# Start of a hybrid decoder block: x fetched first, weights scaled instead of x, half of the scale sums on TensorE

## The chip, the cores and the metric

The kernel runs on one core of a Trainium2 chip. The metric is device time in microseconds (us) for one execution of the whole kernel. Engines: TensorE (PE in the profile: matmuls and transposes; its weight loads are PEld), VectorE (DVE), ScalarE (ACT), GpSimd (POOL) and SyncE (SP). SP does no arithmetic; its queue issues most of the transfers (DMAs) from memory. Every engine runs its own list of instructions in order and waits on semaphores for the others.

## The reference, cut to what matters

One decoder layer on x of 512 tokens by 2048, all fp32. A conditioning vector c makes six rows of 2048 numbers; two of them act on the first normalisation:

```python
mod = (silu(c) @ w_ada + b_ada)                  # w_ada: 2048 x 12288
shift1, scale1, gate1, shift2, scale2, gate2 = split(mod, 6)
h = rms_norm(x, norm1_w) * (1.0 + scale1) + shift1
proj = h @ w_in                                  # w_in: 2048 x 7168
# aq, ak, av (attention), gq, gf, gi, gg (gated recurrence) are columns of proj;
# attention and recurrence, output projection, residual, and an MLP of width 8192 follow
```

So the first large product needs the row scale1 (a product of a vector with a 2048 x 2048 matrix), the norm of every token of x, and x with its features on the partitions.

## The kernel before, in words

The 2048 features are 16 tiles of 128, counted by k; two neighbouring k are a pair, named by its first, k0. Every fp32 operand of a large matmul is split into a rounded high part (fp32r) and the remainder, and a product is made of three matmuls: high by high, high by low, low by high. `_split` does it for weights (L39 on ACT the high part whi, L40 on DVE the low part wlo); the parts of x are hhi and hlo.

The columns of `w_in` are taken in groups. The first group is 512 columns from 4096 (the forget gate) and 256 from 3072 (gq), six 128-column tiles, accumulated over the 16 k in six PSUM banks: 18 matmuls of 128x512 for each k. The second group (`first_groups(4096 + 512, 3072 + 256, ...)`) is the same shape. In both, x carries only the scale; the shift is added later through its own product with `w_in` (`shift_through`). From the third group on, x carries scale and shift, and TensorE's order is written out by hand; that part is outside the change.

What has to be there before the first group:

- g1c, the column form of norm1_w * (1 + scale1). It is made in eight blocks of 256 columns (two k each) by `mod_cols`: `gemv` fetches the block's 2048x256 piece of `w_ada` in eight DMAs on SP (L125) and DVE multiplies the sixteen k pieces by sc = silu(c) and adds them up in two accumulators (L130 for the first two, L132 for fourteen). `to_cols` transposes them (L152, tile pc) and ACT sums over the former partitions (L155); L170 and L172 on DVE add the bias and form the product. Block b serves k = 2b and 2b + 1.
- x: sixteen 128x512 tiles xs (L262 on SP), squares (L271 on ACT, L268 on DVE), the root (L218 on DVE, L219 on POOL), the scaling by rx (L284 ACT, L286 DVE), transposes on TensorE (L290) and ACT's copy out of PSUM (L292), which gives the tiles xnT.
- `scaled(k)`: ACT multiplies xnT[k] by g1c (L342) and rounds it to hhi (L343), DVE makes hlo (L344).

`first_groups` goes over the pairs: `scale_block(k0)` (the weighted sums of the *next* block and `scaled` for both k), then `load_w` (L195, one DMA of 512 KB and one of 256 KB on SP), the splits and the matmuls (`ch_mm`, L213 to L215). At the last pair, `shift_start` begins the vector products of the shift in the background (`bg_step`). In this part the order of the instructions on each engine is made by a scheduler from dependences and priorities, not by the order of the text.

Of the kernel before, what the change touches and what calls it, by code (L numbers as in the profile page):

```python
# [8 lines left out]
F32 = mybir.dt.float32  # L9
# [3 lines left out]
ALU = mybir.AluOpType  # L13
# [21 lines left out]
def _split(nc, pool, src, n=512, eng=None):  # L35

    hi = pool.tile([P, 512], F32R, name="whi", tag="whi")[:, 0:n]
    lo = pool.tile([P, 512], F32R, name="wlo", tag="wlo")[:, 0:n]
    nc.scalar.copy(hi, src)  # L39
    _split.low = (eng or nc.vector).tensor_tensor(lo, src, hi.bitcast(F32), op=ALU.subtract)  # L40
    return hi, lo
# [3 lines left out]
def hybrid_block(ctx, tc, x, c, positions, norm1_w, w_ada, b_ada, w_in, q_norm_w, k_norm_w,  # L45
# [30 lines left out]

    crow = ca.tile([P, P], F32, name="crow", tag="rows")
    nc.sync.dma_start(crow[0:NK], c[0].rearrange("(r p) -> r p", p=P))
    nc.sync.dma_start(crow[NK:2 * NK], norm1_w[0].rearrange("(r p) -> r p", p=P))
    nc.sync.dma_start(crow[2 * NK:P], b_ada[0].rearrange("(r p) -> r p", p=P))  # L80
# [6 lines left out]
    sc = const.tile([P, NK], F32, name="sc")  # L87
# [30 lines left out]
    def gemv(view, vec, col0, n=512, early=False):  # L118
# [72 lines left out]
    def load_w(view, k0, c0, n=512, eng=None, ahead=True, raws=None, behind=False, cast_behind=False):  # L191
        with tc.high_priority() if ahead else ExitStack():
# [5 lines left out]
            with tc.issue_after(evacuated[0].ins) if cast_behind and evacuated else ExitStack():  # L198
                return [_split(nc, wr, raw[:, j], n, eng if j else None) for j in range(2)]
# [51 lines left out]
    hhi, hlo, spare = [], [], []  # L251


    first_scale = mod_cols(1, 0, g1c, n1c, 256, True)
    for _ in range(8):
        next(first_scale)
    xs = [[slot("xs") for _ in range(4)] for _ in range(NT)]
    ssx = sm.tile([P, NT, 4], F32, name="ssx", bufs=1)
    rx = sm.tile([P, NT], F32, name="rx", bufs=1)
    for q in range(4):  # L260
        for ti in range(NT):
            nc.sync.dma_start(xs[ti][q], x_t[:, ti, q * 512:(q + 1) * 512])  # L262
    for q in range(4):
        for ti in range(NT):
            jk = work("jk")
            with tc.issue_after(sc_ready.ins), tc.issue_after(sig_ready.ins):
                if q == 3 and ti % 2:
                    dve.tensor_tensor_reduce(jk, xs[ti][q], xs[ti][q], op0=ALU.mult, op1=ALU.add, scale=1.0, scalar=0.0,  # L268
                                             accum_out=ssx[:, ti, q:q + 1])
                else:  # L270
                    act.activation(jk, xs[ti][q], AF.Square, accum_out=ssx[:, ti, q:q + 1])  # L271
    dve.tensor_reduce(rx, ssx, axis=AX.X, op=ALU.add)
    rstd_of(rx, rx, NT, 1.0 / D)
    run_all(first_scale)
    second_scale = mod_cols(1, 1, g1c, n1c, 256, True)
    spare.extend((hp0, hp1)[k % 2].tile([P, 512], F32, name="araw", tag=f"{c}{k}")
                 for k in range(8, NK) for c in ("hi", "lo"))
    for _ in range(8):
        next(second_scale)
    xnT = []  # L280
    for q in range(4):
        for ti in range(NT):
            if q == 0 and ti % 2 == 0:
                act.activation(xs[ti][q], xs[ti][q], AF.Copy, scale=rx[:, ti:ti + 1])  # L284
            else:
                dve.tensor_scalar(xs[ti][q], xs[ti][q], rx[:, ti:ti + 1], None, op0=ALU.mult)  # L286
# [1174 lines left out]
```

## Time and profile before

| | us |
|---|---|
| median of three runs | 2255.97 (2255.27 to 2257.48) |
| the profiled execution | 2254.72 |
| its span, first to last instruction | 2252.8 |
| PE busy, of the span | 2205.3 (98%) |
| DVE busy | 1807.0 (80%) |
| ACT busy | 1096.5 (49%) |
| POOL busy | 440.5 (20%) |
| first matmul of the first group | 37.24 |
| first matmul of the second group | 121.82 |

The profile is of one execution; its own time is 1.25 us below the median. Busy shares over 2250 us say little about the first 122, so the stretches of that part are read for themselves. "Idle before, releaser" at a row's end names what the engine waited for. The last three numbers of a row of the windows table are the granted TensorE clock (1.00 is full speed, 2.4 GHz), the busy share of the DMA engines and the GB/s that they moved.

### The profile page before, as it was taken

Reading aid. Unit: us, or ns where it says so; the run is one execution under the profiler, and the core shown is the slowest. Engines: PE = TensorE matmul, PEld = TensorE weight load, DVE = VectorE, ACT = ScalarE, POOL = GpSimd, SP = SyncE. Lnnn points to the kernel's source line nnn. Section 1 sums busy time; section 2 is a strip of 40 time slices with the busy share of each in tenths; the row PEclk is TensorE's granted clock in tenths of the full one; section 3 lists DMA queues with packets and bytes.
Section 4 is the critical chain, followed back from the end, with each engine's and each line's share of the span. In section 5 each row is a group of like instructions: output and inputs, shape, how many; then the busy total and the mean of one; then the engine's idle time right before and its main releaser. Section 6 shows DMA issues by size and latency. Waiting matters only on the chain.

```text
span 2252.8 us, 33043 instructions
## 1 busy us (share of the span) xinstructions
PE 2205.3 (98%) x11769; PEld 1823.7 (81%) x11769; DVE 1807.0 (80%) x2765; ACT 1096.5 (49%) x1950; POOL 440.5 (20%) x664
## 2 busy tenths in 40 slices
PE   4999999999999999999999999999999999999999
PEld 3788888888888888888888888888888888888887
DVE  6998878677976566778658988998897779967878
ACT  5555345443453564457545565565654333443332
POOL 1000022000210000003232322232332222222221
PEclk9999999999999999999999999999999999999999
DMA  9797655556555248738879789889989987998884
GB/s 322 261 330 263 212 182 161 172 187 211 174 182 170 76 157 293 259 110 287 319 283 361 294 295 387 317 299 354 345 287 358 372 316 258 341 348 315 307 294 165
DMA packets 262581, 598.30 MB, mean 266 GB/s; under 512 B 23220, under 2 KB 43968, under 8 KB 262416
## 3 DMA queue, kind: packets, MB, share of 16 engines
q1 hardware_dynamic: 186800, 332.54, 43.4%
q0 software_dynamic: 70720, 254.21, 30.7%
q10 hardware_dynamic: 4896, 9.44, 1.3%
q8 instruction: 93, 1.52, 0.3%
q14 instruction: 72, 0.59, 0.1%
HBM read 518.49 MB, written 77.61 MB: 265 GB/s over the span
## 4 chain that ended last, share of the span: by engine, by line
PE 79%; DVE 7%; issue 6%; DMA 6%; POOL 1%; ACT 1%; SPq 0%; POOLq 0%; DVEq 0%; ACTq 0%
PE f L1219 12%; PE f L1217 12%; PE f L1218 12%; PE prj L205 8%; PE prj L207 8%; PE prj L206 8%; PE f L215 2%; PE f L214 2%; PE f L213 2%; PE prj L213 2%; PE prj L214 2%; PE prj L215 2%; DMA f_lod<-fs 1%; DMA Fl<-f_lod 1%; DVE acc L132 1%
## 5 line engine op out<-in xcount | busy, mean ns | idle before, releaser
L1201 ACT CAST vhi<-raw 128x1024 fp32r<-128x1024 f32 x392 | 413.3, 1055 | 519.2 <-PE f L1219 408.8
L1202 DVE TENSOR_TENSOR vlo<-raw,vhi 128x1024 fp32r<-128x1024 f32 x392 | 476.2, 1224 | 139.6 <-ACT vhi L1201 139.2
L1219 PE MATMUL f<-vhi,Fl 128*128 128x512 f32 x1376 | 536.0, 390 | 0.8 <-DMA Fl<-f_lod 0.8
L1218 PE MATMUL f<-vlo,Fh 128*128 128x512 f32 x1376 | 536.3, 390 | 0.5 <-DVE vlo L1202 0.4
L1217 PE MATMUL f<-vhi,Fh 128*128 128x512 f32 x1376 | 536.3, 390 | 0.0
L39 ACT CAST whi<-wraw 128x512 fp32r<-128x512 f32 (+1 forms) x368 | 219.5, 602 | 418.9 <-PE prj L207 273.7
L40 DVE TENSOR_TENSOR wlo<-wraw,whi 128x512 fp32r<-128x512 f32 (+1 forms) x368 | 245.5, 672 | 165.1 <-ACT whi L39 157.3
L205 PE MATMUL prj<-whi,hi 128*128 128x512 f32 x896 | 360.0, 402 | 0.6 <-ACT aq L414 0.5
L207 PE MATMUL prj<-whi,lo 128*128 128x512 f32 x896 | 350.3, 391 | 0.1
L206 PE MATMUL prj<-wlo,hi 128*128 128x512 f32 x896 | 349.4, 390 | 0.0
L1218 PEld LDWEIGHTS f<-vlo,Fh 128*128 128x128 f32 x1376 | 258.4, 188 | 55.1 <-DVE vlo L1202 2.1
L1219 PEld LDWEIGHTS f<-vhi,Fl 128*128 128x128 f32 x1376 | 258.4, 188 | 54.8 <-DMA Fl<-f_lod 1.2
L1217 PEld LDWEIGHTS f<-vhi,Fh 128*128 128x128 f32 x1376 | 258.4, 188 | 53.3
L1185 DVE TENSOR_TENSOR raw<-raw,raw 128x1024 f32<-128x1024 f32 x224 | 271.0, 1223 | 3.4 <-DMA raw<-in_w_ff_dram 3.0
L132 DVE SCALAR_TENSOR_TENSOR acc<-araw,sc,acc 128x512 f32<-128x512 f32 (+1 forms) x392 | 251.0, 677 | 24.3 <-DMA araw<-in_w_ada_dram 23.8
L207 PEld LDWEIGHTS prj<-whi,lo 128*128 128x128 f32 x896 | 168.2, 188 | 36.7 <-DVE lo L247 0.6
L205 PEld LDWEIGHTS prj<-whi,hi 128*128 128x128 f32 x896 | 168.4, 188 | 35.1 <-ACT ak L414 0.9
L206 PEld LDWEIGHTS prj<-wlo,hi 128*128 128x128 f32 x896 | 168.6, 188 | 32.6
L1163 POOL DMA_DIRECT2D Fh<-f_hid x112 | 79.0, 705 | 426.9 <-PE f L1219 409.3
L215 PE MATMUL f<-hi,wlo 128*128 128x512 f32 x256 | 100.0, 391 | 1.1 <-DVE wlo L40 1.1
L213 PE MATMUL f<-hi,whi 128*128 128x512 f32 x256 | 100.4, 392 | 0.0
L214 PE MATMUL f<-lo,whi 128*128 128x512 f32 x256 | 99.7, 390 | 0.0
(311 smaller groups left out, 2905.8 us busy)
## 6 DMA issues: line engine op xcount, KB each, us to landing
raw<-in_w_ff_dram SPq DMA_DIRECT2D x224, 512.0 KB, 10.5
araw<-in_w_ada_dram SPq DMA_DIRECT2D x384, 256.0 KB, 4.5
Fh<-f_hid POOLq DMA_DIRECT2D x112, 512.0 KB, 6.8
Fl<-f_lod POOLq DMA_DIRECT2D x112, 512.0 KB, 8.1
wraw<-in_w_in_dram SPq DMA_DIRECT2D x104, 512.0 KB, 4.9
Fh<-h_hid POOLq DMA_DIRECT2D x60, 512.0 KB, 6.4
Fl<-h_lod POOLq DMA_DIRECT2D x60, 512.0 KB, 7.7
f_hid<-part POOLq DMA_DIRECT2D x48, 512.0 KB, 7.2
```

What stands on the lines that cost most here:

```text
L39: nc.scalar.copy(hi, src)
L40: _split.low = (eng or nc.vector).tensor_tensor(lo, src, hi.bitcast(F32), op=ALU.subtract)
L132: dve.scalar_tensor_tensor(acc, raw[:, k - k0], vec[:, k:k + 1], acc, op0=ALU.mult, op1=ALU.add)
L205: pe.matmul(banks[ti], lhsT=hi[:, ts], rhs=whi, start=first, stop=False)
L206: pe.matmul(banks[ti], lhsT=hi[:, ts], rhs=wlo, start=False, stop=False)
L207: pe.matmul(banks[ti], lhsT=lo[:, ts], rhs=whi, start=False, stop=last)
L1185: dve.tensor_tensor(dst, a, b, op=ALU.subtract)
L1201: cast_done.append(act.copy(hi, src))
L1202: split_done.append(dve.tensor_tensor(lo, src, hi.bitcast(F32), op=ALU.subtract))
L1217: pe.matmul(banks[t], lhsT=fh[u][a][:, ts], rhs=whi[:, a], start=first, stop=False)
L1218: pe.matmul(banks[t], lhsT=fh[u][a][:, ts], rhs=wlo[:, a], start=False, stop=False)
L1219: pe.matmul(banks[t], lhsT=fl[u][a][:, ts], rhs=whi[:, a], start=False, stop=end)
```

## The change

- **x first.** The three small loads of c, norm1_w and the bias go to ACT's queue. SP's first sixteen issues are x, then block 0, pair 0, block 1, pair 2, blocks 2 to 7. The pairs from 4 on are issued on POOL's queue.
- **Weights scaled, x not.** `_split` takes a scale: ACT rounds weight times g1c[k] (L43 of the new kernel), DVE makes the low part with one scalar_tensor_tensor (L44). x goes into the matmuls of both first groups without g1c; `shifted` applies scale and shift to it later.
- **Sums on TensorE.** Blocks 0, 1, 3 and 5 are *summed*: sc stands in the first of 32 columns of a zeroed operand scz, and sixteen matmuls (128x32 by 128x256, fp32) accumulate the k pieces in four strips of 32 partitions of one bank; ACT copies it, two transposes follow (L819), and DVE reduces. Blocks 2, 4, 6 and 7 are *gathered*: sixteen passes on DVE as before (L834, L836), then the old `to_cols` (now L159, L162).
- **Written order.** In this stage PE, SP, ACT and DVE follow the order of the text. For each pair: the parts of x of the next pair, the DVE passes of a gathered next block, the 18 matmuls of the first k, for a summed next block its 16 matmuls, 12 matmuls of the second k, the transposes of the next block's sum (`next_scale`), the last six matmuls, the splits of the next pair's weights. Tiles 8 to 15 of x are transposed at k0 = 2 and 6.
- A Sigmoid on a zeroed tile is run first, and one background piece list is started with 16 steps at the end where there were 12.

The diff, without lines that only rename or carry over:

```diff
-def _split(nc, pool, src, n=512, eng=None):
+def _split(nc, pool, src, n=512, eng=None, scale=None):
 
     hi = pool.tile([P, 512], F32R, name="whi", tag="whi")[:, 0:n]
     lo = pool.tile([P, 512], F32R, name="wlo", tag="wlo")[:, 0:n]
-    nc.scalar.copy(hi, src)
-    _split.low = (eng or nc.vector).tensor_tensor(lo, src, hi.bitcast(F32), op=ALU.subtract)
+    if scale is None:
+        nc.scalar.copy(hi, src)
+        _split.low = (eng or nc.vector).tensor_tensor(lo, src, hi.bitcast(F32), op=ALU.subtract)
+    else:
+        nc.scalar.activation(hi, src, AF.Copy, scale=scale)
+        _split.low = nc.vector.scalar_tensor_tensor(lo, src, scale, hi.bitcast(F32), op0=ALU.mult, op1=ALU.subtract)
...
-    nc.sync.dma_start(crow[0:NK], c[0].rearrange("(r p) -> r p", p=P))
-    nc.sync.dma_start(crow[NK:2 * NK], norm1_w[0].rearrange("(r p) -> r p", p=P))
-    nc.sync.dma_start(crow[2 * NK:P], b_ada[0].rearrange("(r p) -> r p", p=P))
+    act.dma_start(crow[0:NK], c[0].rearrange("(r p) -> r p", p=P))
+    act.dma_start(crow[NK:2 * NK], norm1_w[0].rearrange("(r p) -> r p", p=P))
+    act.dma_start(crow[2 * NK:P], b_ada[0].rearrange("(r p) -> r p", p=P))
...
-                return [_split(nc, wr, raw[:, j], n, eng if j else None) for j in range(2)]
+                return [_split(nc, wr, raw[:, j], n, eng if j else None, None if gain is None else gain[:, k0 + j:k0 + j + 1])
+                        for j in range(2)]
...
-            wt = load_w(win_v, k0, c_f, ahead=False)
-            wc = load_w(win_v, k0, c_q, 256, None, ahead=False)
+            wt = load_w(win_v, k0, c_f, ahead=False, gain=g1c)
+            wc = load_w(win_v, k0, c_q, 256, None, ahead=False, gain=g1c)
...
-    def scale_block(k0):
-        if k0 == 0:
-            run_all(second_scale)
-        elif k0 < 14:
-            run_all(mod_cols(1, k0 // 2 + 1, g1c, n1c, 256, True))
-        for k in (k0, k0 + 1):
-            scaled(k)
...
-    def scaled(k):
-        for l, t in zip((hhi, hlo), pair(k)):
-            l.append(t)
-        act.activation(xnT[k], xnT[k], AF.Copy, scale=g1c[:, k:k + 1])
-        act.copy(hhi[k], xnT[k])
-        dve.tensor_tensor(hlo[k], xnT[k], hhi[k].bitcast(F32), op=ALU.subtract)
-
     def shifted(k):
-        act.activation(hhi[k], xnT[k], AF.Identity, bias=s1c[:, k:k + 1])
-        act.activation(xnT[k], xnT[k], AF.Identity, bias=s1c[:, k:k + 1])
+        for d in (hhi[k], xnT[k]):
+            act.activation(d, xnT[k], AF.Identity, scale=g1c[:, k:k + 1], bias=s1c[:, k:k + 1])
...
+    def first_stage(c_f, c_q):
+
+        order = mybir.EngineType
+        with tc.manual_schedule(engines={order.PE, order.SP, order.Activation, order.DVE}):
+            return first_steps(c_f, c_q)
...
+        scz = slot("scz").rearrange("p (k m) -> p k m", m=32)
+        pool.memset(scz, 0.0)
...
+        on_pe = (0, 1, 3, 5)
...
+        def fetch_pair(k0):
+            wraws[k0] = []
+            for c, n in ((c_f, 512), (c_q, 256)):
+                raw = wr.tile([P, 2, n], F32, name="wraw", tag="raw", bufs=4)
+                (pool if k0 > 2 else nc.sync).dma_start(raw, win_v[:, k0:k0 + 2, c:c + n])
+                wraws[k0].append(raw)
+
+        def split_w(k):
+            parts[k] = [_split(nc, wr, raw[:, k % 2], raw.shape[2], None, g1c[:, k:k + 1]) for raw in wraws[k - k % 2]]
+
+        def split_x(ks):
+            for k in ks:
+                hl = pair(k)
+                hhi.append(hl[0])
+                hlo.append(hl[1])
+                split_to(hl, xnT[k])
...
+        def turn_x(q, j, tag="bg"):
+            pt = bank("ptx", tag=tag)
+            for ti in range(NT):
+                pe.transpose(pt[:, ti * P:(ti + 1) * P], xs[ti][q][:, j * P:(j + 1) * P], ident)
+            t = slot("xnT")
+            (dve.tensor_copy if q == 1 else act.copy)(t, pt)
+            xnT.append(t)
+
+        def summed(b, rounds):
+            if b not in accs:
+                accs[b] = bank("gp")
+            for r in rounds:
+                for j in range(4):
+                    k = 4 * r + j
+                    pe.matmul(accs[b][32 * j:32 * j + 32, 0:256], lhsT=scz[:, k], rhs=raws[b][k // 2][:, k % 2],
+                              start=r == 0, stop=r == 3)
+
+        def summed_out(b):
+            t = work("acc")[:, 0:256]
+            act.copy(t, accs[b][:, 0:256])
+            pc = bank("pc")
+            for j in range(2):
+                pe.transpose(pc[:, j * P:(j + 1) * P], t[:, j * P:(j + 1) * P], ident)
+            dve.tensor_reduce(g1c[:, 2 * b:2 * b + 2], pc[:, 0:256].rearrange("p (j a m) -> p j a m", j=2, m=32)[:, :, :, 0],
+                              axis=AX.X, op=ALU.add)
+            finish_scale(b)
+
+        def finish_scale(b):
+            d = g1c[:, 2 * b:2 * b + 2]
+            dve.tensor_tensor(d, d, bcol[:, NK + 2 * b:NK + 2 * b + 2], op=ALU.add)
+            mod_cols.last = dve.scalar_tensor_tensor(d, d, 1.0, n1c[:, 2 * b:2 * b + 2], op0=ALU.add, op1=ALU.mult)
+
+        def gathered(b):
+            accs[b] = [work("acc")[:, 0:256] for _ in range(2)]
+            for k in range(NK):
+                raw, acc = raws[b][k // 2][:, k % 2], accs[b][k % 2]
+                if k < 2:
+                    dve.tensor_scalar(acc, raw, sc[:, k:k + 1], None, op0=ALU.mult)
+                else:
+                    dve.scalar_tensor_tensor(acc, raw, sc[:, k:k + 1], acc, op0=ALU.mult, op1=ALU.add)
+
+        def gathered_out(b):
+            for _ in to_cols(accs[b], g1c[:, 2 * b:2 * b + 2]):
+                pass
+            finish_scale(b)
...
+        fetch_block(0)
+        fetch_pair(0)
+        scale_x(0, (0, 1))
+        summed(0, (0, 1))
+        turn_x(0, 0, "mm")
+        turn_x(0, 1, "mm")
+        scale_x(1, ())
+        split_x((0,))
+        summed(0, (2, 3))
+        summed_out(0)
+        turn_x(0, 2, "mm")
+        turn_x(0, 3, "mm")
+        fetch_block(1)
+        fetch_pair(2)
+        for j in range(4):
+            turn_x(1, j, "mm")
+        split_w(0)
+        split_x((1,))
+        split_w(1)
+        fetch_block(2)
+        split_x((2, 3))
+
+        bt = [bank("prj", tag="mm") for _ in range(4)]
+        bc = [bank("prc") for _ in range(2)]
+
+        def dense(k, between=None):
+            fine, coarse = parts.pop(k)
+            first, last = k == 0, k == NK - 1
+            for n, (hs, w) in enumerate(((hhi, 0), (hlo, 0), (hhi, 1))):
+                for banks, ws in ((bt, fine), (bc, coarse)):
+                    for j in range(len(banks)):
+                        pe.matmul(banks[j], lhsT=ws[w][:, j * P:(j + 1) * P], rhs=hs[k], start=first and n == 0,
+                                  stop=last and n == 2)
+                if n == 1 and between:
+                    between()
+
+        def next_scale(b):
+            if b in on_pe:
+                summed_out(b)
+            elif b < 8:
+                gathered_out(b)
+
+        for k0 in range(0, NK, 2):
+            b = k0 // 2 + 1
+            if k0 + 4 < NK:
+                fetch_pair(k0 + 4)
+            if k0 in (0, 4):
+                scale_x(2 + k0 // 4, range(NT))
+            if 0 < k0 < NK - 2:
+                split_x((k0 + 2, k0 + 3))
+            if b < 8 and b not in on_pe:
+                gathered(b)
+            dense(k0)
+            if b in on_pe:
+                summed(b, range(4))
+            if k0 in (2, 6):
+                turn_x(2 + k0 // 6, 0)
+                turn_x(2 + k0 // 6, 1)
+            dense(k0 + 1, lambda: next_scale(b))
+            if k0 in (2, 6):
+                turn_x(2 + k0 // 6, 2)
+                turn_x(2 + k0 // 6, 3)
+            if b + 2 < 8:
+                fetch_block(b + 2)
+            for k in (k0 + 2, k0 + 3):
+                if k < NK:
+                    split_w(k)
+        for _ in range(16):
+            bg_step()
+        return bt, bc
...
-    bt, bc = first_groups(4096, 3072, scale_block, shift_start)
+    xnT = []
+    bt, bc = first_stage(4096, 3072)
```

The order of the instructions on three engines follows from it. First SP at the start of the program, before (araw is a piece of `w_ada`, wraw a pair of `w_in`, xs is x):

```order
L78 DMA crow<-in_c_dram 16x128
L79 DMA crow<-in_norm_w_dram 16x128
L80 DMA crow<-in_b_ada_dram 96x128
L125 DMA araw<-in_w_ada_dram 128x2x256 x8
L262 DMA xs<-in_x_dram 128x512 x16
L125 DMA araw<-in_w_ada_dram 128x2x256 x8
L195 DMA wraw<-in_w_in_dram 128x2x512
L195 DMA wraw<-in_w_in_dram 128x2x256
L125 DMA araw<-in_w_ada_dram 128x2x256 x8
```

and of the changed kernel:

```order
L845 DMA xs<-in_x_dram 128x512 x16
L760 DMA araw<-in_w_ada_dram 128x2x256 x8
L767 DMA wraw<-in_w_in_dram 128x2x512
L767 DMA wraw<-in_w_in_dram 128x2x256
L760 DMA araw<-in_w_ada_dram 128x2x256 x8
L767 DMA wraw<-in_w_in_dram 128x2x512
L767 DMA wraw<-in_w_in_dram 128x2x256
L760 DMA araw<-in_w_ada_dram 128x2x256 x48
```

x has moved from behind block 0 to the first place; of the pairs only 0 and 2 are left on this queue.

Second DVE, where one block's sum ends and another begins, before (L170 and L172 finish g1c; lo is a low part of x):

```order
L344 TENSOR_TENSOR lo_578<-xnT,hi_577 128x512
L132 SCALAR_TENSOR_TENSOR acc<-araw,sc,acc 128x256
L344 TENSOR_TENSOR lo_583<-xnT,hi_582 128x512
L170 TENSOR_TENSOR g1c<-g1c,bcol 128x2
L132 SCALAR_TENSOR_TENSOR acc<-araw,sc,acc 128x256
L130 TENSOR_SCALAR acc<-araw,sc 128x256 x2
L132 SCALAR_TENSOR_TENSOR acc<-araw,sc,acc 128x256
L172 SCALAR_TENSOR_TENSOR g1c<-g1c,n1c 128x2
L132 SCALAR_TENSOR_TENSOR acc<-araw,sc,acc 128x256 x8
L344 TENSOR_TENSOR lo_687<-xnT,hi_686 128x512
```

and of the changed kernel from the last splits of pair 2 (k0 = 2) to the first of pair 4:

```order
L44 SCALAR_TENSOR_TENSOR wlo<-wraw,g1c,whi 128x512
L44 SCALAR_TENSOR_TENSOR wlo<-wraw,g1c,whi 128x256
L255 TENSOR_TENSOR lo_544<-xnT,hi_543 128x512
L255 TENSOR_TENSOR lo_548<-xnT,hi_547 128x512
L834 TENSOR_SCALAR acc<-araw,sc 128x256 x2
L836 SCALAR_TENSOR_TENSOR acc<-araw,sc,acc 128x256 x14
L826 TENSOR_TENSOR g1c<-g1c,bcol 128x2
L827 SCALAR_TENSOR_TENSOR g1c<-g1c,n1c 128x2
L44 SCALAR_TENSOR_TENSOR wlo<-wraw,g1c,whi 128x512
L44 SCALAR_TENSOR_TENSOR wlo<-wraw,g1c,whi 128x256
```

Before, the passes of a block are mixed with low parts and the finishing steps; now all low parts of the step stand ahead, the sixteen passes in one piece, and the finishing steps after them.

Third TensorE around the transposes of a gathered block (L152 before, L159 now), before, in the step of k0 = 4:

```order
L213 MATMUL prj<-hi_686,whi 128x512 x4
L152 MATMUL pc<-ident,acc 128x128
L214 MATMUL prj<-lo_687,whi 128x512 x4
L152 MATMUL pc<-ident,acc 128x128 x3
L215 MATMUL prj<-hi_686,wlo 128x512 x4
L213 MATMUL prc<-hi_686,whi 128x512
L214 MATMUL prc<-lo_687,whi 128x512
```

and of the changed kernel, in the second k of k0 = 2:

```order
L883 MATMUL prj<-hi_428,whi 128x512 x4
L883 MATMUL prc<-hi_428,whi 128x512 x2
L883 MATMUL prj<-lo_429,whi 128x512 x4
L883 MATMUL prc<-lo_429,whi 128x512 x2
L159 MATMUL pc<-ident,acc 128x128 x4
L883 MATMUL prj<-hi_428,wlo 128x512 x4
L883 MATMUL prc<-hi_428,wlo 128x512 x2
L800 MATMUL ptx<-ident,xs 128x128 x8
L883 MATMUL prj<-hi_543,whi 128x512 x4
```

Before, the four transposes are spread among the matmuls of the step's first k; now they stand as one behind the twelve matmuls with hi and lo of the second k, with six matmuls and eight transposes of x behind them.

## Rows read from the trace of the kernel before

**Rows 1.** Windows table of core 0: stretch, length, busy us (instructions), clock, DMA:

```profile
0.00:37.24 37.24, 7.33 (x37) 5.74 (x37) 19.21 (x54) 17.51 (x46) 9.63 (x24) 1.00 0.93 303
...
52.94:62.84 9.90, 9.90 (x37) 8.00 (x37) 9.90 (x26) 4.71 (x11) 0.00 (x0) 0.83 1.10 354
94.66:121.82 27.16, 27.16 (x115) 21.77 (x115) 21.38 (x67) 15.85 (x31) 0.00 (x0) 0.94 0.29 85
121.82:187.00 65.18, 65.18 (x296) 53.87 (x295) 60.47 (x109) 37.38 (x86) 5.29 (x9) 1.00 0.95 339
187.00:2252.80 2065.80, 2055.27 (x11090) 1701.69 (x11088) 1648.81 (x2392) 992.32 (x1712) 425.55 (x631) 1.00 0.75 263
```

**Rows 2.** Waits of PE in 0 to 190 us: total, times, longest:

```profile
PE ptx L290 <- ACT xs L284: 12.8, 1, 12.8
...
PE prj L213 <- ACT hi L343: 7.1, 4, 4.1
```

**Rows 3.** Timeline of SP's DMA issues, 0 to 35 us:

```profile
2.11 5.63 SPq L125 DMA_DIRECT2D araw<-in_w_ada_dram  x8
7.78 13.11 SPq L262 DMA_DIRECT2D xs<-in_x_dram  x16
```

**Rows 4.** Timeline of the x-norm chain on ACT:

```profile
25.57 0.63 ACT L271 ACTIVATE jk<-xs 128x512 f32<-128x512 f32 x1 [0.42 <-DMA xs<-in_x_dram]
...
29.16 1.33 ACT L284 ACTIVATE xs<-xs,rx 128x512 f32<-128x512 f32 x2 [2.87 <-POOL rx L219]
```

**Rows 5.** Timeline of DVE: weighted sums of block 0:

```profile
13.75 2.46 DVE L132 SCALAR_TENSOR_TENSOR acc<-araw,sc,acc 128x256 f32<-128x256 f32 x6 [1.40 <-DMA araw<-in_w_ada_dram]
```

**Rows 6.** Groups by line and shape, 0 to 122 us: busy, mean ns:

```profile
L40 DVE TENSOR_TENSOR wlo<-wraw,whi 128x512 fp32r<-128x512 f32 x18 | 12.6, 699 | 2.4 <-ACT whi L39 2.1 <-PE pc L152 0.3
...
L342 ACT ACTIVATE xnT<-xnT,g1c 128x512 f32<-128x512 f32 x16 | 10.8, 718 | 5.2 <-DVE g1c L172 5.2
...
L292 ACT COPY xnT<-ptx 128x512 f32<-128x512 f32 x16 | 8.4, 615 | 2.8 <-PE ptx L290 2.8
L132 DVE SCALAR_TENSOR_TENSOR acc<-araw,sc,acc 128x512 f32<-128x512 f32 x10 | 7.7, 774 | 0.0
...
L40 DVE TENSOR_TENSOR wlo<-wraw,whi 128x256 fp32r<-128x256 f32 x17 | 7.2, 434 | 1.2 <-ACT whi L39 1.2
...
L155 ACT ACTIVATE pc<-pc 128x256 f32<-128x256 f32 x16 | 5.9, 367 | 2.5 <-PE pc L152 2.2
...
L155 ACT ACTIVATION_READ_ACCUMULATOR pc<-pc 128x1 f32 x16 | 3.0, 190 | 0.0
```

**Rows 7.** Timeline of PE: steady matmuls, then sixteen transposes:

```profile
117.74 0.39 PE L213 MATMUL prj<-hi,whi 128*128 128x512 f32 x1
117.96 0.39 PE L214 MATMUL prj<-lo,whi 128*128 128x512 f32 x1
...
43.57 1.91 PE L290 MATMUL ptx<-ident,xs 128*128 128x128 f32 x16
```

**Rows 8.** Timeline of PE: 128x32 strips, 128x256 fp32 matmuls and neighbours:

```profile
252.37 0.39 PE L207 MATMUL prj<-whi,lo 128*128 128x512 f32 x1
252.69 0.46 PE L585 MATMUL pA<-gq,kk 128*32 128x32 f32 x32
252.96 1.02 PE L585 MATMUL pA<-z 128*32 128x32 f32 x96
253.91 0.51 PE L205 MATMUL prj<-whi,hi 128*128 128x512 f32 x1
...
277.10 1.02 PE L685 MATMUL pE<-z 128*128 128x256 f32 x4
```

**Rows 9.** Timeline of PE after two waits; windows row of a slow stretch:

```profile
52.94 1.70 PE L213 MATMUL prj<-hi,whi 128*128 128x512 f32 x4 [1.97 <-ACT hi L343]
...
94.66 2.08 PE L213 MATMUL prj<-hi,whi 128*128 128x512 f32 x4 [4.06 <-ACT hi L343]
...
53.40:56.70 3.30, 3.30 (x10) 2.51 (x9) 3.30 (x10) 0.62 (x4) 0.00 (x0) 0.50 1.10 349
```

More of the change, by code (lines that the diff above doesn't have):

```diff
@@ L75, in hybrid_block @@
     pool.memset(mhalf, -0.5)
+    sc = const.tile([P, NK], F32, name="sc")
+    dve.memset(sc, 0.0)
+    act.activation(sc, sc, AF.Sigmoid)
     crow = ca.tile([P, P], F32, name="crow", tag="rows")
-    nc.sync.dma_start(crow[0:NK], c[0].rearrange("(r p) -> r p", p=P))
-    nc.sync.dma_start(crow[NK:2 * NK], norm1_w[0].rearrange("(r p) -> r p", p=P))
-    nc.sync.dma_start(crow[2 * NK:P], b_ada[0].rearrange("(r p) -> r p", p=P))
+    act.dma_start(crow[0:NK], c[0].rearrange("(r p) -> r p", p=P))
+    act.dma_start(crow[NK:2 * NK], norm1_w[0].rearrange("(r p) -> r p", p=P))
+    act.dma_start(crow[2 * NK:P], b_ada[0].rearrange("(r p) -> r p", p=P))
     ps_c = bank("ps_c")
@@ L86, in hybrid_block @@
     dve.tensor_copy(bcol, ps_c[:, 2 * NK:P])
-    sc = const.tile([P, NK], F32, name="sc")
     sig_ready = act.activation(sc, ps_c[:, 0:NK], AF.Sigmoid)
@@ L122, in gemv @@
         for k0 in range(0, NK, nk):
-            raw = spare.pop(0) if early and spare else slot("araw") if early else gv.tile([P, 512], F32, name="araw", bufs=4)
+            raw = slot("araw") if early else gv.tile([P, 512], F32, name="araw", bufs=4)
             raw = raw.rearrange("p (k n) -> p k n", n=n)
-            asked[0] = nc.sync.dma_start(raw, view[:, k0:k0 + nk, col0:col0 + n])
+            with tc.issue_after(asked[0].ins) if early or view is win_v else ExitStack():
+                asked[0] = nc.sync.dma_start(raw, view[:, k0:k0 + nk, col0:col0 + n])
             for k in range(k0, k0 + nk):
@@ L189, in hybrid_block, with load_w @@
     evacuated = []
-    def load_w(view, k0, c0, n=512, eng=None, ahead=True, raws=None, behind=False, cast_behind=False):
+    def load_w(view, k0, c0, n=512, eng=None, ahead=True, raws=None, behind=False, cast_behind=False, gain=None):
         with tc.high_priority() if ahead else ExitStack():
@@ L250, in hybrid_block @@
         pair(i)
[L251 to L286, printed above, removed]
-        for j in range(4):
-            pt = bank("ptx")
-            for ti in range(NT):
-                pe.transpose(pt[:, ti * P:(ti + 1) * P], xs[ti][q][:, j * P:(j + 1) * P], ident)
-            t = slot("xnT")
-            act.copy(t, pt)
-            xnT.append(t)
+    hhi, hlo = [], []
     def first_groups(c_f, c_q, before, after):
@@ L308, in first_groups @@
         return bt, bc
-    def scale_block(k0):
-        if k0 == 0:
-            run_all(second_scale)
-        elif k0 < 14:
-            run_all(mod_cols(1, k0 // 2 + 1, g1c, n1c, 256, True))
-        for k in (k0, k0 + 1):
-            scaled(k)
-    def shift_start(k0):
-        if k0 == 14:
-            for _ in range(12):
-                bg_step()
     shift_done, behind = set(), []
```

36 lines of the change are left out of this document (added).

## The prediction, made before the change was run

> **What bounds the kernel now.** I read the stretches first. From 187 us to the end TensorE is busy 2055.27 of 2065.80 us, and from 94.66 to 187 us it is never idle [rows 1]. So the change, which touches the first 190 us, is worth what it moves T1, the start of the second column group (121.82 us before), plus what it makes the second group wait. The list of TensorE's waits comes next: 12.8 us for the normalised x before the first transposes, and 7.1 us in four waits for a scaled, rounded x [rows 2]. Then the stretches again: from 52.94 to 62.84 us, one step of two k, DVE is busy 9.90 of 9.90 us [rows 1]. TensorE needs only 36 matmuls .2275 us apart in a step, 8.19 us [rows 7]; DVE's sixteen weighted sums, splits and low parts fill the step. So the start has two bounds: x arrives late, and then DVE is the wall, since each block of g1c costs it sixteen passes.
>
> **The start.** SP issued eight ada fetches at 2.11 us and x only from 7.78 us [rows 3]; x's last square began at 25.57 us and the scaling by rx at 29.16 [rows 4]. Now the three small loads are ACT's and x is first on SP: it is issued 7.0 us earlier, so the last square starts at 18.5 us. By bytes it comes to the same: 2.1 MB less ahead of it, at the stretch's 303 GB/s [rows 1], are 6.9 us. With the chain of before, 3.6 us, x can be scaled at 22.1. Block 0 now lies behind x; eight issues took 5.6 us [rows 3], so it lands at 24.1. Eight strip matmuls behind it cost .9 (next part), ACT's copy .5, the transposes .3, three small DVE steps .6: g1c(0) at 26.4. ACT still copies two transposed tiles of x (.615 each [rows 6]) and then rounds the scaled weights, .72 by the scaling row L342 [rows 6]: 28.4. The four PSUM banks also hold transposed x: twenty-four transposes at .12 [rows 7] from 25.9 and DVE's last copy, .6, free the fourth at 29.4, and the fourth matmul waits for it. I take 28.8 us for the first dense matmul, 27.3 to 30.3 as its bounds. Before, it was 37.24, and with x's transposes between matmuls.
>
> **A summed step (blocks 1, 3, 5).** Sixteen fp32 matmuls of 128x32 on 256 columns replace sixteen DVE passes. Before has no such matmul. The nearest rows: a 128x256 fp32 matmul leaves two records, four of them in 1.02 us with the last .38 long, so .21 apart [rows 8]; thirty-two of those are 6.8 us one behind the other. But 128 records of 128x32 on 32 columns, dealt round the four strips as here, took 1.22 us from 252.69 to 253.91 [rows 8], 9.5 ns each, where 32 of 256 columns' .21 would be 27 ns: the strips ran about three to four at once. So the sums cost 1.7 us (four at once) to 6.8 (none). I take 1.8, near the row that has strips. To this come .2 of transposes and .2 of gaps: the first strip started .32 behind the matmul ahead of it instead of .23 [rows 8]. The Trainium skill says in "TensorEngine Tiling (Array Packing)", Key Properties, that changing the tiling mode drains TensorE; the rows agree, but the drain they show is .1 us at a switch, so the rule speaks against this change by less than 1 us over four blocks. DVE then has only a reduce and two small steps between the transposes and the weights' rounding: .6 + .72 against six matmuls of cover, 1.37. A summed step is 8.2 + 1.8 + .4 = 10.4 us.
>
> **A gathered step (blocks 2, 4, 6, 7).** Here the written order decides. DVE first makes the four low parts of this step's weights and two of x, and only then takes the sixteen passes of the next block. The low parts are now scalar_tensor_tensor, which for 128x512 is .774 against .699 for the old form [rows 6]; laid into each other four take 2.2 us and x's two 1.3. Six passes took 2.46 us, .39 apart [rows 5], so sixteen are 6.2. The sum is ready 9.8 us into the step. TensorE comes to its transposes, written between the low-x and the low-weight part of the second k, after 30 matmuls, at 6.8 us, and waits there: 3.0 us. Behind it in TensorE's order are six matmuls and all later ones. Then a chain with little cover: transposes .6, two accumulating copies on ACT .37 + .19 each [rows 6], so 1.1, two DVE steps .4, the rounding .72: the next step starts at 12.6 us, while the six matmuls end at 11.7. That holds for k0 = 10 and 12. For k0 = 2 and 6 sixteen transposes of x (1.91 for sixteen [rows 7]) are in the step; eight of them stand behind the six matmuls, and ACT must copy their two tiles ahead of the rounding: 9.8 + .5 + 1.4 + 1.0 + .2, then 1.2 of copies overlapping the second four transposes by .6, then .72, gives 14.1 us.
>
> **The sum.** 28.8 + 3 x 10.4 + 2 x 14.1 + 2 x 12.6 + 8.2 (last step) = 121.6 us, against 121.82. To it comes the clock. Before, after waits of 1.97 and 4.06 us TensorE was granted .50, 1.2 GHz of 2.4, for 3.3 us [rows 9], and lost 1.65. Each gathered step now has such a wait, 2 to 3 us. If all four fall: 1.65 each in the two steps with transposes, where TensorE feeds ACT, and .5 each in the other two, where the chain over ACT and DVE hides most: 4.3. The other two of the four waits, 7.1 - 4.06 - 1.97 = 1.1 us together [rows 2, 9], brought no fall; the waits here lie nearer to the longer two, but are split by six matmuls, and I charge half, 2.1, with 0 to 4.3 as bounds. T1 is 123.7, 1.9 later than before: eight microseconds won at the start go back in the steps.
>
> The second group: it scales its weights too, and x is unscaled; on ACT the scaled rounding hides under matmuls (ACT is busy 37.38 of 65.18 us [rows 1]). DVE was busy 60.47 of 65.18 there. Thirty-two low parts cost .05 to .075 more, 2.1 us; twelve 512-wide passes of the shift (.7 each, 8 us) that before had done ahead of T1 (ten of them are the row L132 of 128x512 [rows 6]) can now start only after the last gathered block, and some 5 us of DVE are free there before T1. So about 65.5 us of work in 65.2 to 67: it just fits, and I count it at nothing; if the last low parts come late it costs up to 5. The moves of weights to POOL's queue and of SP's order cost nothing as I read it: each pair is asked two steps, over 20 us, ahead of its use, and no queue stands between; what late transfers would cost shows first as TensorE waiting for a rounding, and its bounds are 0 and 2.
>
> So the profiled execution of 2254.72 us (2252.8 of span, 1.92 around it) becomes 2256.6. The median of the three runs shown is 1.25 above it, and I give the time on that scale: 2257.9, rounded to 2258.
>
> **The rivals.**
> Strips one behind the other. The matmul rows of 32 columns could be fast only for being short. Then each summed step grows by 5.0 us and block 0's last half by some 2: 17 us, 2275. For it: 256 columns in strips were never run here. Against: 9.5 ns a record cannot be had with one strip at 27 ns. The same page of the Trainium skill states that different tiles load and multiply in parallel, which also speaks against it. Chance .10.
> DVE bounds the second group. The place is TensorE's wait for low weights of group two. It decides if the shift's twelve passes all fall behind T1: 60.5 + 2.1 + 8 = 70.6 us of work in 65.2. It costs about 5 on top: 2263. For it: DVE had 4.7 us to spare. Against: the last step leaves it some. Chance .15.
> The early start is kept. If DVE's passes hide under TensorE, because DVE or the chain over ACT is quicker than I count, and a gathered step takes 10.5 instead of 12.6 to 14.1, that is 2 x 2.1 + 2 x 3.6 = 11.4, and with no clock lost, T1 is 110.2: 11.6 before the old one, 2244. For it: before, DVE did the same passes and low parts in a step of 9.9 us [rows 1]. Against: those passes had been spread over the step by a scheduler and begun a block ahead; here sixteen stand in one piece behind six low parts. Chance .18.
> The change doesn't reach its early start: block 0's data or banks come as late as 32 us. Then 3 more, 2261. Chance .05.
>
> **How the numbers follow.** About .2 per cent, 4.5 us, is what a measurement of this kernel can tell from no change. My own case has .52; its bounds (start -1.5 to +1.5, clock -2.1 to +2.2, strips 0 to +1.5) give 2254 to 2263, with .80 of it within 4.5 us of before, .15 above and .05 below. Faster is then .03 and .17 of the kept start, .20. Slower is .08, .10 of the strips, .09 of the second group and .02 of the late start, .29. The same is .51. The range: below, most of the way to the kept start, 2247; above, all but the serial strips, 2267.
>
> **What would show it.** Right: the first square of x near 6 us, the first dense matmul near 29; summed steps of 10 to 11 us and gathered ones of 12 to 14; TensorE's list of waits headed by the transposes pc waiting for acc, four times 2 to 3 us; slow clock behind them; T1 at 121 to 126. Wrong: strips over .1 us apart; no wait for acc; TensorE waiting for wlo after T1; a weight transfer as a releaser.

## The result: 0.4 per cent slower, and where it went

The changed kernel took 2266.83 us in the median of five runs (2263.68 to 2268.9), the kernel before 2257.48 beside it: a ratio of 1.004, interval 1.0026 to 1.0055, 9.35 us slower. Forecast were 2258 and, as likeliest, no change that a measurement tells; the range reached from 2247 to 2267. The profiled execution took 2263.68 us, 8.96 more than that of before.

The stretches of the changed kernel, as in [rows 1]: the start, a gathered step (k0 = 2), a summed step (k0 = 4), the gathered step k0 = 10, the second group, and the 41 us behind it.

```profile
0.00:29.48 29.48, 9.37 (x67) 5.76 (x68) 8.40 (x27) 14.84 (x37) 10.04 (x25) 1.00 0.95 306
...
41.17:54.84 13.67, 11.11 (x57) 8.78 (x57) 9.80 (x25) 6.17 (x15) 1.44 (x2) 1.00 1.06 342
54.84:65.70 10.86, 10.78 (x70) 7.71 (x70) 3.98 (x10) 5.98 (x12) 1.45 (x2) 1.00 0.95 302
...
90.23:102.72 12.49, 10.37 (x41) 7.85 (x41) 9.88 (x25) 4.20 (x11) 1.45 (x2) 0.89 0.80 283
...
123.34:188.50 65.16, 65.16 (x294) 53.91 (x293) 60.78 (x120) 36.54 (x77) 4.04 (x8) 1.00 0.90 311
188.50:230.00 41.50, 35.33 (x151) 28.89 (x151) 40.65 (x71) 28.26 (x58) 0.53 (x1) 0.92 0.80 283
```

The first dense matmul stands at 29.48 us (37.24 before), the second group starts at 123.34 (121.82 before): forecast were 28.8 and 123.7. So the first stage gives back its lead as the prediction said, and 1.5 of the 9.0 us are lost by there. The second group is as full as before, 65.16 of 65.16. The other 7.5 us arise in the last row: TensorE is busy 35.33 of 41.50 us, at a clock of .92. The same stretch of before, as far behind the start of its second group, has no idle time:

```profile
186.98:228.48 41.50, 41.50 (x188) 34.41 (x187) 35.33 (x59) 22.63 (x50) 0.00 (x0) 1.00 0.74 257
```

TensorE's waits up to 200 us, the columns as in [rows 2]:

```profile
PE gp L811 <- DVE ssx L785: 12.1, 1, 12.1
...
PE pc L159 <- DVE acc L836: 6.3, 4, 2.1
PE prj L883 <- ACT whi L43: 3.1, 3, 1.3
```

The four waits for acc were foreseen, at 3 us each; they are 1.2 to 2.1. TensorE around one of them, from the start of the dense part to the end of step k0 = 2:

```profile
29.48 2.01 PE L883 MATMUL prj<-hi,whi 128*128 128x512 f32 x4
...
34.07 0.61 PE L883 MATMUL prc<-hi,wlo 128*128 128x512 f32 x2
34.62 1.93 PE L811 MATMUL gp<-araw,scz 128*32 128x256 f32 x32
36.48 1.20 PE L883 MATMUL prj<-hi,whi 128*128 128x512 f32 x4
...
50.38 0.85 PE L159 MATMUL pc<-ident,acc 128*128 128x128 f32 x4 [1.21 <-DVE acc L836]
...
54.84 1.20 PE L883 MATMUL prj<-hi,whi 128*128 128x512 f32 x4 [1.34 <-ACT whi L43]
```

The reader sees three things. The sixteen strip matmuls leave 32 records in 1.93 us, .05 apart: four strips at once, 1.8 had been forecast [rows 8]. The second of the two matmuls at 34.07 starts at 34.30, and the first strip .32 behind it instead of .23. (The Trainium skill states in "TensorEngine Tiling (Array Packing)", Key Properties, that changing the tiling mode drains TensorE; this trace agrees, with about .1 us at the switch.) The transposes of a gathered block wait 1.21 us; TensorE comes to them 8.0 us into the step, since eight transposes of x stand ahead of them, and not at the 6.8 us from which the forecast wait of 3.0 was reckoned for every gathered step. And the next step waits again, 1.34 us, for ACT's rounding behind the transposes of x. DVE in the same step:

```profile
41.15 2.21 DVE L44 SCALAR_TENSOR_TENSOR wlo<-wraw,g1c,whi 128x512 fp32r<-128x512 f32 x4 [0.84 <-DMA araw<-in_w_ada_dram]
43.27 1.29 DVE L255 TENSOR_TENSOR lo<-xnT,hi 128x512 fp32r<-128x512 f32 x2
44.48 0.61 DVE L834 TENSOR_SCALAR acc<-araw,sc 128x256 f32<-128x256 f32 x2
45.00 5.63 DVE L836 SCALAR_TENSOR_TENSOR acc<-araw,sc,acc 128x256 f32<-128x256 f32 x14
```

Low parts until 44.5, the sixteen passes in one piece until 50.6: 9.5 us from the start of the step, 9.8 forecast.

What the prediction had not seen comes at 212 us, in the third group. There TensorE waits for DVE, in the changed kernel:

```profile
212.15 0.39 PE L215 MATMUL prj<-whi,lo 128*128 128x512 f32 x1
218.71 1.11 PE L159 MATMUL pc<-ident,acc 128*128 128x128 f32 x4 [6.17 <-DVE acc L153]
```

```profile
217.98 0.67 DVE L153 TENSOR_TENSOR acc<-acc 128x512 f32<-128x512 f32 x1
```

and before, the same transposes (L152, then L159) and the same addition ahead of them (L146, then L153):

```profile
216.27 0.60 PE L152 MATMUL pc<-ident,acc 128*128 128x128 f32 x4
```

```profile
206.85 0.69 DVE L146 TENSOR_TENSOR acc<-acc 128x512 f32<-128x512 f32 x1
```

These are the transposes of `shift_through(4096)`, the shift's product with the weights of the first group. Counted from the start of the second group, DVE ended the addition at 85.7 us before and at 95.3 in the changed kernel, 9.6 later; TensorE came to the transposes at 94.45 before and at 89.2 now (212.54), 5.3 earlier. The 8.7 us to spare became a wait of 6.17. The first row below is DVE from the start of group two to that addition; the second is TensorE behind the wait, where the clock stood at .50 for 4.3 us:

```profile
123.34:218.65 95.31, 89.20 (x401) 73.46 (x399) 90.94 (x171) 58.10 (x118) 4.57 (x9) 0.99 0.91 317
218.65:222.95 4.30, 4.24 (x12) 3.55 (x13) 3.45 (x7) 3.03 (x9) 0.00 (x0) 0.50 1.05 382
```

The wait and half of this stretch, 6.2 + 2.1 = 8.3 us, are what the third group loses. Its first strips show it:

```profile
262.59 0.46 PE L532 MATMUL pA<-gq,kk 128*32 128x32 f32 x32
```

They stand 139.25 us behind the start of group two, 130.87 before [rows 8], 8.4 later. Up to the end of the kernel .8 of it comes back: the time behind the start of group two grew by 7.58 us.

DVE's stretch up to that addition before:

```profile
121.82:207.54 85.72, 85.72 (x387) 70.90 (x386) 78.35 (x139) 50.14 (x114) 5.29 (x9) 1.00 0.97 347
```

DVE has 12.6 us more work in it (90.94 against 78.35) and idles 3.0 less, which is the 9.6. The groups of the weighted sums in these stretches, before and after (count, busy, mean ns):

```profile
L132 DVE SCALAR_TENSOR_TENSOR acc<-araw,sc,acc 128x512 f32<-128x512 f32 x46 | 33.4, 755 | 0.0
...
L132 DVE SCALAR_TENSOR_TENSOR acc<-araw,s1c,acc 128x512 f32<-128x512 f32 x15 | 10.8, 745 | 0.0
```

```profile
L139 DVE SCALAR_TENSOR_TENSOR acc<-araw,sc,acc 128x512 f32<-128x512 f32 x52 | 37.6, 749 | 0.0
L139 DVE SCALAR_TENSOR_TENSOR acc<-araw,s1c,acc 128x512 f32<-128x512 f32 x20 | 14.1, 733 | 0.0
...
L44 DVE SCALAR_TENSOR_TENSOR wlo<-wraw,g1c,whi 128x512 fp32r<-128x512 f32 x14 | 10.4, 744 | 1.3 <-PE prc L223 0.8 <-issue 0.6
```

Eleven passes more (one of them is cut by the start of the stretch), 7.5 us, because DVE had done twelve of the shift's passes ahead of group two before and seven now, and because the second product of the shift runs five further. Low parts of the weights make some 2.3 us more, and the small steps of the positions, most of which DVE had done ahead of group two before, some 3.6; the other groups are slightly shorter.

### The profile page after: what moved, and what is told of

Read it like the earlier page. It is cut to its first block, busy times and chain, and to the rows that moved or that the text cites. A ratio compares the mean times of both kernels' runs of the same rounds, so it can differ in the third digit from the quotient of the medians.

```text
span 2261.9 us, 33188 instructions
## 1 busy us (share of the span) xinstructions
PE 2215.9 (98%) x11889; PEld 1825.1 (81%) x11889; DVE 1788.2 (79%) x2707; ACT 1093.6 (48%) x1923; POOL 449.9 (20%) x677
## 4 chain that ended last, share of the span: by engine, by line
PE 82%; DMA 6%; DVE 5%; issue 5%; POOL 1%; ACT 1%; SPq 0%; ACTq 0%; POOLq 0%; DVEq 0%
PE f L1351 13%; PE f L1349 13%; PE f L1350 13%; PE prj L213 8%; PE prj L215 8%; PE prj L214 8%; PE f L223 3%; PE f L221 2%; PE f L222 2%; PE prj L223 1%; PE prj L222 1%; PE prj L221 1%; DMA araw<-in_w_ada_dram 1%; DMA Fl<-f_lod 1%; PE pho L643 1%
## 5 line engine op out<-in xcount | busy, mean ns | idle before, releaser
L40 ACT CAST whi<-wraw 128x512 fp32r<-128x512 f32 x304 | 187.1, 621 | 363.1 <-PE prj L215 277.8
L41 DVE TENSOR_TENSOR wlo<-wraw,whi 128x512 fp32r<-128x512 f32 x304 | 209.2, 692 | 156.4 <-ACT whi L40 151.3
L139 DVE SCALAR_TENSOR_TENSOR acc<-araw,sc,acc 128x512 f32<-128x512 f32 x280 | 201.8, 748 | 21.0 <-DMA araw<-in_w_ada_dram 20.3
```

Of the source, the lines that this page charges most:

```text
L139: dve.scalar_tensor_tensor(acc, raw[:, k - k0], vec[:, k:k + 1], acc, op0=ALU.mult, op1=ALU.add)
```

## The experiments

**Where the step counter stands.** The changed kernel takes 16 background steps at the end of the first stage, before took 12. In the third group TensorE's order is written with two background steps for every k, so four steps are two k, 24 matmuls.

```diff
-        for _ in range(16):
+        for _ in range(12):
             bg_step()
```

> The changed kernel with 12 background steps at the end of the first stage instead of 16. Theory A: its loss sits in one wait of 6.2 us in the third group, TensorE's transposes pc for the shift's product with w_in, and in 1.7 us of slow clock behind it. Two parts make the wait: the sixteen steps put these transposes four steps, two k or 24 matmuls of .2275 us, 5.5 us earlier in TensorE's written order, and DVE comes to their input 9.6 us later after the start of group two than before, against 8.7 us that it had to spare. Taking the four steps back moves the transposes 5.5 us later: the wait falls to about 1 us, the clock stays, the kernel gets 6 to 7 us faster: 2257 in the profiled run, about 3 us above the kernel before. Theory B: DVE's backlog alone decides, and the wait comes back at the next thing that DVE makes: TensorE still waits 4 to 6 us for DVE between 190 and 260 us, and the time stays within 2 us of the changed kernel's.

Measured: 2257.62 us, ratio 1.0006 (.9998 to 1.0015). The wait is gone, and up to 420 us no other stands in its place; the transposes and the addition ahead of them:

```profile
218.31 0.60 PE L159 MATMUL pc<-ident,acc 128*128 128x128 f32 x4
```

```profile
216.28 0.70 DVE L153 TENSOR_TENSOR acc<-acc 128x512 f32<-128x512 f32 x1
```

DVE ends 1.3 us before TensorE comes, where a wait of 1 us was expected. The four steps tell on DVE too: the addition ends 93.1 us behind the start of group two (123.84), and not 95.3; so they move TensorE 5.3 us forward and DVE 2.2 us back. Theory A holds in this: of the ratio's .40 per cent .34 hang on four steps in a loop count, some 8 us. What is left is within the interval of nothing; up to the third group the profile shows it as the later start of group two. The profiled execution, 2260.33 us where 2257 were expected, is the slowest of the eleven.

**The same count in the kernel before.**

```diff
-            for _ in range(12):
+            for _ in range(16):
                 bg_step()
```

> The kernel before with 16 background steps instead of 12 at the last pair of the first group, nothing else. Theory A (two parts make the wait in the third group): the transposes of the shift's product come 5.5 us earlier in TensorE's written order, DVE had 8.7 us to spare for them there, so no wait, and the time stays within 2 us of before. Rival (the four steps alone cost it): a wait of TensorE for acc of some 4 to 6 us in the third group and a slow clock behind it, 5 to 8 us slower than before.

Measured: 2255.28 us beside 2256.27, ratio .9999 (.999 to 1.0008). The transposes moved 5.6 us forward and found their input long done:

```profile
210.68 0.60 PE L152 MATMUL pc<-ident,acc 128*128 128x128 f32 x4
```

```profile
202.56 0.69 DVE L146 TENSOR_TENSOR acc<-acc 128x512 f32<-128x512 f32 x1
```

So the count alone costs nothing. DVE's addition moved 4.2 us forward too, counted from the start of group two, but at its old place it would still have been 3.2 us early (8.7 - 5.5). It took both: the transposes moved up and DVE's backlog.

**All blocks on TensorE.**

```diff
-        on_pe = (0, 1, 3, 5)
+        on_pe = tuple(range(8))
```

> The changed kernel with all eight scale blocks summed on TensorE. Theory A: the four waits of TensorE for acc (6.3 us together) go, each of these steps gains 1.9 us of strip matmuls and loses the chain over two accumulating copies; group two starts at about 118.5 instead of 123.3. DVE still begins with the shift's pieces only behind the last low weights of the stage, 6 us ahead of group two, so the wait of 6 us in the third group stays: about 2259 in the profiled run, 4 to 5 us less than the changed kernel. Theory B: DVE's 25 us of passes in the first stage are what makes the shift late; without them the wait in the third group goes too and the time is 2250 to 2253.

Measured: 2267.08 us, ratio 1.0048 (1.0035 to 1.006), the changed kernel's time. Waits up to 420 us:

```profile
PE pc L159 <- DVE acc L153: 6.9, 1, 6.9
PE prj L883 <- ACT whi L43: 2.7, 2, 1.3
PE ptx L800 <- ACT xnT L802: 1.4, 2, 0.7
```

The wait in the third group stayed, as theory A has it, though DVE is rid of 25 us of passes; theory B falls. But group two starts at 123.64, not at 118.5: this part of theory A's sum failed. The steps k0 = 10 and 12 did fall to 10.9 and 11.0 us (82.59 to 123.64 for four steps, the last of 8.3); but the first dense matmul came 1.0 us later, at 30.49, and the steps with transposes of x grew from 13.7 to 14.8, since strips, transposes and ACT's copies now stand in one row there (the two waits for xnT and the two of 1.35 for whi).

**The passes one step earlier.**

```diff
+            ahead = {0: 2, 4: 4, 8: 6, 10: 7}.get(k0)
+            if ahead is not None:
+                gathered(ahead)
-            if b < 8 and b not in on_pe:
-                gathered(b)
```

> The changed kernel with the sixteen DVE passes of blocks 2, 4, 6 and 7 written one step earlier (in the steps k0 = 0, 4, 8, 10), the transposes where they were. Theory A: DVE idles 6 to 8 us in each summed step, so the passes fit there, TensorE no longer waits for acc, and a gathered step falls by 2 to 3 us; group two starts at 112 to 115; the wait of 6 us in the third group stays as it is, since DVE's pieces of the shift still follow the last low weights: 2253 to 2256 in the profiled run. Theory B: the bound in these steps is the chain behind the transposes (accumulating copies, two small steps, rounding), and DVE would only be late with the low parts of the weights: group two starts within 3 us of 123.3.

Measured: 2267.53 us, ratio 1.0048 (1.0035 to 1.0061); group two at 125.57 instead of 112 to 115. That is within theory B's 3 us of 123.3, but not by its chain: the transposes wait for DVE no longer, and three of the four gathered steps fell, k0 = 6, 10 and 12 to 12.1, 10.5 and 9.8 us. The loss is elsewhere. DVE and TensorE in the step k0 = 0:

```profile
42.48 2.47 DVE L836 SCALAR_TENSOR_TENSOR acc<-araw,sc,acc 128x256 f32<-128x256 f32 x6 [0.66 <-DMA araw<-in_w_ada_dram]
44.86 0.16 DVE L820 TENSOR_REDUCE g1c<-pc 128x2 f32<-128x8 f32 x1
```

```profile
46.27 2.08 PE L883 MATMUL prj<-hi,whi 128*128 128x512 f32 x4 [5.17 <-ACT whi L43]
```

The passes waited for block 2's transfers, the reduce of block 1 (L820) stood behind them in DVE's order, and TensorE waited 5.17 us for weights scaled by it, with a slow clock behind (.81 in the step k0 = 2, 14.7 us). In the step k0 = 4 the data are there, but the low parts of x wait 2.16 us for ACT, the reduce behind the passes comes only 11.6 us into the step, and TensorE waits 2.23 us for the weights: the wait had changed its owner. In the step k0 = 8, with no such wait of DVE, the sixteen passes did fit:

```profile
86.10:96.97 10.87, 10.81 (x70) 7.71 (x70) 9.96 (x26) 3.53 (x8) 1.44 (x2) 1.00 0.64 203
```

It takes 10.87 us, as in the changed kernel. The wait in the third group stayed, 5.7 us.

**The weights' queue.**

```diff
-                (pool if k0 > 2 else nc.sync).dma_start(raw, win_v[:, k0:k0 + 2, c:c + n])
+                nc.sync.dma_start(raw, win_v[:, k0:k0 + 2, c:c + n])
```

> The changed kernel with all pairs of weights issued on SP's queue. Theory A: no transfer is waited for in this stage, so the queue is of no account: within 2 us of the changed kernel. Rival: behind pairs that wait for a free buffer SP's later issues of blocks come late, TensorE or DVE waits for araw, and it is slower by 3 us or more; or POOL's transfers were the slower ones, and it is faster by 3 us or more.

Measured: 2264.16 us, ratio 1.0037 (1.0024 to 1.0051), the changed kernel's within the interval, with its two waits:

```profile
PE pc L159 <- DVE acc L836: 6.3, 4, 2.1
PE pc L159 <- DVE acc L153: 6.1, 1, 6.1
```

The queue is of no account in this stage.

**x first, alone, in the kernel before.** The sixteen fetches of x ahead of block 0's eight, and the three small loads on ACT's queue.

```diff
     first_scale = mod_cols(1, 0, g1c, n1c, 256, True)
-    for _ in range(8):
-        next(first_scale)
...
             nc.sync.dma_start(xs[ti][q], x_t[:, ti, q * 512:(q + 1) * 512])
+    for _ in range(8):
+        next(first_scale)
```

> The kernel before with x fetched ahead of block 0 and the three small loads on ACT's queue, nothing else. Theory A: x comes 6 to 7 us earlier, but block 0 and with it every later block comes as much later to DVE, and DVE's passes are the wall from then on, so group two starts within 2 us of 121.8 and the time stays within 2 us of before. Rival: the first matmul's wait for x was the bound, and an earlier x is kept: group two 5 us or more earlier and the time 2250 or less.

Measured: 2255.65 us, ratio 1.0 (.9991 to 1.0009). TensorE's waits for DVE's first sums and the first dense matmul:

```profile
PE pc L152 <- DVE acc L132: 22.1, 3, 19.9
```

```profile
40.58 1.20 PE L213 MATMUL prj<-hi,whi 128*128 128x512 f32 x4
```

The wait for x fell from 12.8 us [rows 2] to 4.5, but the one for block 0 grew from 11.8 to 19.9, and the first dense matmul even stands at 40.58 instead of 37.24; group two starts at 121.55. x first is worth nothing by itself here. That it pays with block 0 summed on TensorE is likely from the changed kernel's 29.48, but no run separates that from the other parts of the change.

**Both lessons together.** Twelve steps, six of them at k0 = 12; block 7 summed too; passes of blocks 2, 4 and 6 in two parts; the transposes six matmuls earlier.

```diff
-        on_pe = (0, 1, 3, 5)
+        on_pe = (0, 1, 3, 5, 7)
...
+        early = {2: 6, 4: 10, 6: 10}
...
+            if b < 8 and b not in on_pe:
+                gathered(b, range(early[b], NK))
             if 0 < k0 < NK - 2:
                 split_x((k0 + 2, k0 + 3))
-            if b < 8 and b not in on_pe:
-                gathered(b)
+            if b + 1 in early:
+                gathered(b + 1, range(early[b + 1]))
+            if k0 == NK - 4:
+                for _ in range(6):
+                    bg_step()
...
-            dense(k0 + 1, lambda: next_scale(b))
-            if k0 in (2, 6):
-                turn_x(2 + k0 // 6, 2)
-                turn_x(2 + k0 // 6, 3)
+            between = {0: lambda: next_scale(b)}
+            if k0 in (2, 6):
+                between[1] = lambda: [turn_x(2 + k0 // 6, j) for j in (2, 3)]
+            dense(k0 + 1, between)
...
-        for _ in range(16):
+        for _ in range(6):
             bg_step()
```

> The changed kernel with 12 background steps (six of them in the step k0 = 12), block 7 summed on TensorE too, the DVE passes of blocks 2, 4 and 6 in two parts (6 or 10 a step ahead, the rest ahead of the low parts of x) and the transposes six matmuls earlier in the second k. Theory A: a step's low parts (3.4 us) with ten passes (3.9) end before TensorE comes to the transposes, and so do the weights' low parts with six passes (2.2 + 2.4), so no wait for acc is left, and twelve matmuls cover the chain behind the transposes: a step with transposes of x 10.7 to 11.5 us instead of 13.7, k0 = 10 about 9 instead of 12.5, k0 = 12 about 10.8 instead of 12.3; group two starts at 112 to 115; DVE has the shift's pieces as early against group two as with 12 steps, so no wait in the third group above 2 us: 2246 to 2250 in the profiled run, faster than both kernels. Rival: DVE's and the transfers' totals are the bound; what TensorE wins before group two it waits for in the third group, and the time stays at 2254 or above.

Measured: 2246.95 us beside 2256.27, ratio .9965 (.9953 to .9978): by the ratio some 8 us faster than the kernel before, and 17 than the changed one (1.004). The first stage, the second group and the 40 us behind it, and TensorE in the step k0 = 2:

```profile
28.60:110.31 81.71, 81.51 (x472) 62.62 (x471) 59.57 (x144) 41.52 (x86) 8.73 (x12) 1.00 0.90 291
110.31:175.50 65.19, 65.19 (x295) 53.95 (x294) 64.06 (x129) 43.64 (x88) 4.48 (x8) 1.00 0.97 344
175.50:215.00 39.50, 39.50 (x180) 32.70 (x179) 35.80 (x61) 22.79 (x49) 0.53 (x1) 1.00 0.79 282
```

```profile
39.95 1.07 PE L884 MATMUL prj<-hi,whi 128*128 128x512 f32 x4
...
46.29 0.60 PE L159 MATMUL pc<-ident,acc 128*128 128x128 f32 x4
...
50.51 1.19 PE L884 MATMUL prj<-hi,whi 128*128 128x512 f32 x4
```

TensorE is busy 81.51 of 81.71 us in the first stage and all the time in the next 105; the transposes wait for nothing; the step with transposes of x takes 10.6 us (39.95 to 50.51) instead of 13.7; group two starts at 110.31, earlier than the 112 to 115 expected. The rival falls: what TensorE wins is not asked back in the third group. Not all of it reaches the end, though: of the 11.5 us by which group two starts earlier the profiled execution keeps 8. The rest is lost some 1078 us behind the start of group two, in the first row below; the second row is the same stretch of before:

```profile
1188.00:1250.00 62.00, 59.45 (x261) 48.49 (x260) 52.85 (x55) 29.77 (x33) 13.86 (x20) 0.97 0.83 302
1200.00:1262.00 62.00, 61.23 (x287) 50.76 (x286) 55.65 (x58) 33.81 (x40) 15.26 (x22) 1.00 0.86 311
```

TensorE waits there 2.2 us for DVE's s in the attention, .6 before, and runs at half the clock behind it. The kernel with 12 steps shows the same; no run tells why DVE is later there.

## Why the prediction was right, and where it was not

- **The time** lies in the range by luck: 2266.83 is .17 us under an upper end that was drawn to hold all but the serial strips, and what cost the time is none of the rivals as they stand there. By the prediction's own measure, .2 per cent, the kernel is slower, which it gave .29, and not the same, .51.
- **The start** held: 29.48 us for 28.8, 37.24 before. The four banks hold the first matmuls, as counted (four in 2.01 us). The first square of x stood at 8.50 us, not near 6, behind sc in ACT's order; it cost nothing, for the last one, which counts, stood at 18.62 (18.5 forecast).
- **The summed step** held: 10.86 and 10.87 us for 10.4 (the first, with the banks' wait in it, 11.69); the strips ran four at once at 1.93 us for 1.8. The rival of serial strips falls.
- **The gathered step** held: 13.67, 13.66, 12.49 and 12.32 us for 14.1 and 12.6. Its account was right too, though the waits were 1.2 to 2.1 us for 3.0 each: the last kernel, which takes the wait and the bare chain away, takes 3 us off such a step.
- **The clock** was charged too high. One of the four waits (2.11 us, at k0 = 10) was followed by a slow stretch, and its step is .2 us longer than the next, whose wait of 1.71 us brought none; 2.1 us were charged. That the sum up to group two came out 0.4 us off is owed in part to errors that cancel: the start and the summed steps were counted 2.9 us too short, the gathered steps and the clock 3.4 too long.
- **The step that failed** is "it just fits, and I count it at nothing" for what follows. The rival "DVE bounds the second group" had the right cause, DVE's shift passes that fall behind T1, but the wrong place: no low weight was late in group two, where DVE was busy 60.78 of 65.16 us and not for 65.5. The rest of its work lay behind: in the 41.50 us after it DVE was busy 40.65, 35.33 before. The queue behind the low parts was the shift's own sum, and its reader stands in the third group, which the prediction took for untouched because TensorE was full there before. Full is not the same as unmoved: the line `range(16)`, which stands in no term of the prediction, shifts transposes by 24 matmuls in an order written by hand. The run with 12 steps has DVE's backlog without the shifted transposes, the run of the kernel before with 16 has the shifted transposes without the backlog, and neither has the wait.
- **The kept start** did not come in this kernel, but the last kernel shows that it was to be had: its T1 is 110.31 us, where that rival had 110.2 for passes hidden under TensorE. That kernel sums block 7 on TensorE too, so the two figures agree more closely than the reasoning earns.

## What to carry to other kernels

A lead on one engine is kept only if the engine behind it gets its work into the same time: look for where the idle time of the helper (here 32 of DVE's 94 us in the first stage) and its backlog stand in its written order. In a hand-written order a count of background steps is a position: before changing it, see which instruction it moves, and how long that instruction's input had been ready. A long piece of helper work that makes something late in one gap can fit in two.

## What was not expected of the hardware

The length of TensorE's wait did not tell whether the clock falls. After 1.97 us it fell to 1.2 GHz of 2.4 before [rows 9], and after 2.11 us here, at k0 = 10:

```profile
100.50:102.90 2.40, 2.40 (x7) 1.59 (x6) 0.61 (x3) 1.95 (x7) 0.00 (x0) 0.50 0.19 73
```

In the kernel with the passes one step earlier a wait of 2.23 us ended at 74.03 us, and the clock stayed:

```profile
74.00:78.00 4.00, 3.98 (x17) 3.30 (x18) 3.42 (x6) 2.42 (x5) 1.44 (x2) 1.00 1.10 359
```

What TensorE had done ahead of the waits differs (in that kernel it had been held up 5.17 us some 28 us earlier); which of it decides was not tried.
